# Moving weight conversions out of the projection stages, and conditioning rows between gate stages, in a two-layer decoder trunk

## The chip, the cores and the metric

One Trainium2 chip, eight cores in two dies (cores 0 to 3 and 4 to 7). Each core computes one of eight batch elements; the cores exchange nothing. The time is that of the slowest core, in microseconds of the device.

A run is in one of two states. In a slow one, a die shows a lower granted TensorE clock than the other and is over 1% longer (or the run is over 1.5% above the fastest of the same kernel). I also use the **undisturbed-die time**: the median span of a die's four cores, where their median granted clock was at least 0.9965, averaged over all such dies of all runs of a kernel on one chip.

## The reference, cut to what matters

```python
D_MODEL, BATCH, SEQ, DEPTH, D_FF = 1024, 8, 4096, 2, 2816
for l in range(DEPTH):
    mod = c_act @ ada_w[l] + ada_b[l]              # 9 vectors of 1024: "conditioning rows"
    sh1, sc1, g1, sh2, sc2, g2, sh3, sc3, g3 = jnp.split(mod, 9, axis=-1)
    y = modulate(rmsnorm(h, norm_g[l, 0]), sh1, sc1)
    h = h + 0.5 * g1 * swiglu(y, ffn1_wg[l], ffn1_wu[l], ffn1_wd[l])
    y = modulate(rmsnorm(h, norm_g[l, 1]), sh2, sc2)
    proj = y @ w_in[l]                             # the projection stage
    ...                                            # gating unit || dilated attention
    h = h + g2 * (mixed @ w_out[l])
    y = modulate(rmsnorm(h, norm_g[l, 2]), sh3, sc3)
    h = h + 0.5 * g3 * swiglu(y, ffn2_wg[l], ffn2_wu[l], ffn2_wd[l])
```

All weights arrive as f32. The kernel uses bf16.

## The kernel before: what the change and the argument touch

The kernel describes its work as a graph of tasks. When the program is built, a list scheduler with a model of the DMA gives each engine a fixed order; on the chip only semaphores hold it. So one moved transfer can change the order of every engine.

```python
def schedule(self, bw=270.0, dlat=2300.0, ...):    # the model: 270 bytes/ns, 2.3 us to land
    ...
    if t.dma:
        far = t.L - hp                             # distance to the deadline
        bl = backlog if far < 12000.0 or now < 100000.0 else 5000.0 if far < 40000.0 else 2500.0
        if pipe[0] - now > bl:                     # modelled backlog: hold this transfer back
            ...
            continue
```

A **conversion** is a DMA from DRAM to DRAM issued by GpSimd, which rounds f32 to bf16. It waits only for a matmul, its gate:

```python
def conv(l, w, spans, gates=True):                 # spread over stretches of TensorE's program time
    items = ([(j, None) for j in range(FC)] if gates else []) + [(None, m) for m in range(KC)]
    ...
        gate = max((k for k in marks if k[0] <= p), key=lambda k: k[0], default=(0, None))[1]
        if j is not None:                          # gate-up weights: 22 per FFN
            G.dma("pool", lambda e, j=j: e.dma_start(out=wguS[l, w, j], in_=wgu_d[l, w, j]), 1572864,
                  writes=[bWG[l, w, j]], name="cvg", pos=p, extra=[gate])
        else:                                      # down weights: 8 per FFN
            G.dma("pool", lambda e, m=m: e.dma_start(out=wdS[l, w, m], in_=wd_d[l, w, m]), 2162688, ...)
```

A **conditioning row** (`cond`) loads 512 KB of `ada_w` and multiplies and sums it on VectorE. In a projection stage TensorE multiplies the normalised rows by `w_in`; beside it the next tiles of h are loaded and normalised. Their squares run on ScalarE, in the same queue as the copies that empty PSUM:

```python
def norm_sum(ht, pos, alts=0):
    ...                                            # each kc: ScalarE, needs the load of ht.b[kc]
    G.op([act(lambda e, sq=sq, hk=hk: e.activation(out=sq, in_=hk, func=AF.Square), 520)],
         reads=[ht.b[kc]], writes=[bq], name="sq", pos=pos)
```

The stages of one layer, with 0, p1, ... as TensorE's program time:

```python
f1.gates((0, 1, 2, 3), ...)      # p1 .. pg   first gates
f1.downs(...); f1.downs(...)     # pg .. p2
mx0.proj(t)  # t = 0..3          # p2 .. p3   first projection stage
fa.gates, fa.downs, ...          # p3 .. p4   gates of tiles 4..7, attention woven in
mx1.proj(t); outproj(...)        # p4 .. p6   second projection stage
fb.gates, fb.downs, ...          # p6 .. p7   second FFN, attention woven in
fc.gates((4, 5, 6, 7), ...)      # p8 .. s1   last gates
```

The softmax here doesn't subtract the row's maximum and nothing guards it: scores larger than these inputs give would overflow.

## Time and profile before

| | before |
|---|---|
| first three timed runs | 4849.5, 5211.1, 5432.4 us |
| profiled run (fast) | 4873.3 us |
| TensorE's waits over 0.1 us, median core | 78.8 us, of which 44.2 before the first projection stage |

The last row is mine: for each two successive matmuls of the trace I take the time from start to start, less the pace of an unbroken stream (215.8 ns for 512 columns; the formula is in the prediction), and sum what exceeds 0.1 us. The median is over the six cores whose traces hold every matmul. This sum is small: 1.6% of the span. The views themselves are shown in the prediction.

Two cautions go with it. The cores of one run differ: the six stand at 71.7 to 81.5 us here. And not all of it is waiting. The clock records of the traces show short stretches, often of 3.4 us, in which a core was granted half its clock (0.5); a matmul of 512 columns then takes 0.21 us more, and the sum counts it.

### The profile page before, as it was taken

How to read it: one execution, taken by the hardware profiler on the slowest of the kernel's cores; microseconds unless marked ns; L12 is line 12 of the kernel's file. 1: busy time of each engine (PE TensorE's matmuls, PEld its weight loads, DVE VectorE, ACT ScalarE, POOL GpSimd, SP SyncE). 2: the span in 40 equal slices, each digit the busy share in tenths (PEclk: the TensorE clock that was granted, in tenths of full speed). 3: DMA queues.
4: the chain of work that ended last, by engine and by line, in shares of the span. 5: the costliest groups of instructions: out<-in, count | busy, mean ns of one | idle time of the engine just before them, and what ended most of it. 6: DMA issues, size and time to landing. Idle time of an engine off the chain costs nothing.

```text
span 4871.8 us, 74168 instructions; the slowest of 8 cores (4820.7 to 4871.8 us)
## 1 busy us (share of the span) xinstructions
PE 4789.6 (98%) x25859; PEld 2257.4 (46%) x25859; DVE 2461.2 (51%) x4088; ACT 2035.0 (42%) x3024; POOL 973.5 (20%) x949
## 2 busy tenths in 40 slices
PE   6999999999999999999999999999999999999998
PEld 2444445444445554444444444444444455544443
DVE  6452566473655473655233326645537544525433
ACT  5112576452755352512211127645537444525311
POOL 0001551212531111300100026312235100122101
PEclk9999999999999999999999999999999999999999
DMA  8888676777575768755721466756665644473314
GB/s 240 169 191 230 166 204 159 191 206 218 172 209 150 200 192 240 218 147 165 249 66 39 120 200 163 208 155 184 149 190 164 185 148 140 123 248 124 136 42 157
DMA packets 370033, 834.80 MB, mean 171 GB/s; under 512 B 148961, under 2 KB 182113, under 8 KB 363234
## 3 DMA queue, kind: packets, MB, share of 16 engines
q1 hardware_dynamic: 352338, 741.56, 49.4%
q0 software_dynamic: 17328, 88.49, 12.1%
q8 instruction: 213, 3.49, 0.3%
q14 instruction: 154, 1.26, 0.1%
HBM read 741.20 MB, written 234.88 MB: 200 GB/s over the span
## 4 chain that ended last, share of the span: by engine, by line
PE 92%; ACT 2%; DMA 2%; DVE 2%; issue 1%; POOL 0%; SPq 0%; DVEq 0%; ACTq 0%; POOLq 0%
PE ps L1002 48%; PE ps L1030 25%; PE ps L1141 9%; PE ps L1467 5%; PE ps L1409 3%; PE ps L1375 2%; DMA arena<-xP 1%; DMA arena<-hS 0%; DVE arena L1206 0%; DVE arena L948 0%; POOL arena L1182 0%; DMA arena<-ada_w 0%; ACT arena L1184 0%; DMA arena<-wdS 0%; PE ps L1234 0%
## 5 line engine op out<-in xcount | busy, mean ns | idle before, releaser
L1002 PE MATMUL ps<-arena 128*128 128x512 bf16 x11264 | 2511.5, 381 | 32.6 <-DMA arena<-wgu 25.0
L1002 PEld LDWEIGHTS ps<-arena 128*128 128x128 bf16 x11264 | 1083.9, 98 | 1312.0 <-issue 86.4
L1030 PE MATMUL ps<-arena 128*128 128x512 bf16 x5632 | 1242.7, 382 | 1.1 <-DMA arena<-wdS 1.1
L1008 ACT ACTIVATE arena<-ps 128x512 f32<-128x512 f32 x704 | 419.7, 597 | 1283.7 <-PE ps L1002 1279.9
L1010 DVE SCALAR_TENSOR_TENSOR arena<-arena,ps 128x512 f32<-128x512 f32 x704 | 481.4, 685 | 771.9 <-ACT arena L1008 770.7
L1030 PEld LDWEIGHTS ps<-arena 128*128 128x128 bf16 x5632 | 550.7, 98 | 665.6 <-issue 47.9
L926 POOL TENSOR_TENSOR arena<-arena 128x512 f32<-128x512 f32 (+2 forms) x351 | 414.2, 1180 | 1218.4 <-ACT arena L919 1116.3
L1034 DVE SCALAR_TENSOR_TENSOR arena<-ps,arena 128x512 f32<-128x512 f32 x256 | 192.1, 751 | 908.3 <-PE ps L1030 899.9
L1015 DVE TENSOR_TENSOR arena<-ps,arena 128x512 bf16<-128x512 f32 x704 | 485.0, 690 | 216.6 <-PE ps L1002 193.3
L1141 PE MATMUL ps<-arena 128*128 128x512 bf16 x2560 | 577.1, 385 | 9.0 <-ACT arena L1225 5.8
L919 ACT ACTIVATE arena<-arena 128x512 bf16<-128x512 f32 x424 | 250.9, 625 | 709.1 <-DVE arena L1034 379.3
L1393 ACT ACTIVATE arena<-ps 128x1024 bf16<-128x1024 f32 (+1 forms) x384 | 344.9, 950 | 308.3 <-PE ps L1375 307.6
L1141 PEld LDWEIGHTS ps<-arena 128*128 128x128 bf16 x2560 | 251.0, 99 | 314.7 <-issue 52.0
L1396 DVE TENSOR_TENSOR arena<-arena 128x1024 bf16<-128x1024 bf16 (+1 forms) x384 | 256.1, 675 | 126.0 <-ACT arena L1393 124.6
L961 ACT ACTIVATE arena<-arena 128x512 bf16<-128x512 f32 x372 | 278.4, 806 | 45.2 <-DVE arena L948 45.1
L1445 POOL TENSOR_TENSOR arena<-arena 64x512 bf16<-64x512 f32 x128 | 163.8, 1280 | 623.1 <-ACT arena L1440 600.0
L948 DVE TENSOR_TENSOR arena<-arena 128x512 f32<-128x512 f32 x384 | 268.3, 747 | 35.0 <-ACT arena L934 32.0
L1467 PE MATMUL ps<-arena 128*128 128x512 bf16 x1024 | 230.1, 386 | 0.0
L1425 DVE TENSOR_TENSOR arena<-ps,arena 128x512 f32<-128x512 f32 x256 | 175.5, 685 | 65.2 <-PE ps L1409 57.5
L1409 PEld LDWEIGHTS ps<-arena 128*128 128x128 bf16 x2736 | 173.6, 98 | 63.4 <-issue 7.1
L1213 POOL TENSOR_TENSOR arena<-arena 128x512 bf16<-128x512 f32 x128 | 167.9, 1320 | 174.8 <-DVE arena L1204 120.2
L1409 PE MATMUL ps<-arena 128*128 128x128 bf16 x2736 | 194.4, 219 | 1.9 <-DVE arena L1010 0.9
(79 smaller groups left out, 2112.7 us busy)
## 6 DMA issues: line engine op xcount, KB each, us to landing
arena<-wguS SPq DMA_DIRECT2D x242, 512.0 KB, 5.7
arena<-hS SPq DMA_DIRECT2D x204, 512.0 KB, 6.8
arena<-wdS SPq DMA_DIRECT2D x128, 704.0 KB, 5.9
arena<-ada_w SPq DMA_DIRECT2D x144, 512.0 KB, 5.9
hS<-arena SPq DMA_DIRECT2D x224, 256.0 KB, 5.8
wguS<-wgu POOLq DMA_DIRECT2D x66, 512.0 KB, 7.8
hS<-arena SPq DMA_DIRECT2D x64, 512.0 KB, 4.3
arena<-xP SPq DMA_DIRECT2D x48, 512.0 KB, 9.0
```

Of the source, the lines that this page charges most:

```text
L926: f = lambda e, a=a, sq=sq, out=out: e.tensor_tensor(out=out, in0=a, in1=sq, op=ALU.add)
L948: f = lambda e, hk=hk, u=u: e.tensor_tensor(out=u, in0=hk, in1=rs, op=ALU.mult)
L961: ga = act(lambda e, hk=hk, A=A, sh=sh, o=o: e.activation(out=o, in_=hk, func=AF.Identity, scale=A, bias=sh), 725)
L1002: mate = main([(lambda e, kc=kc, half=half, bk=bk, y=y, gu=gu: e.matmul(bank(bk), lhsT=gu[:, half, kc, :], rhs=y[:, kc, :], start=(kc == 0 ...
L1008: G.op([act(lambda e, sg=sg, gb=gb: e.activation(out=smv[sg.i], in_=bank(gb), func=AF.Tanh, scale=0.5), 490, "tanh")], reads=[gb], writes= ...
L1010: G.op([dve(lambda e, sg=sg, gb=gb: e.scalar_tensor_tensor(out=smv[sg.i], in0=smv[sg.i], scalar=1.0, in1=bank(gb), op0=ALU.add, op1=ALU.mu ...
L1015: G.op([dve(lambda e, sg=sg, ub=ub, o=o: e.tensor_tensor(out=o, in0=bank(ub), in1=smv[sg.i], op=ALU.mult), 610)], reads=[ub, sg], writes=[ ...
L1030: main([(lambda e, j=j: e.matmul(bank(bk), lhsT=wd[:, j, :], rhs=a[:, j, :], start=(j == 0), stop=(j == FC - 1)), [bwd, ba[j]], MM) for j ...
L1141: ins.append((lambda e, lhs=lhs, rhs=rhs, kc=kc: e.matmul(bank(bk), lhsT=lhs, rhs=rhs, start=(kc == 0), stop=(kc == KC - 1)), rd + [by[kc] ...
L1393: return e.activation(out=cut(pT, 0), in_=cut(ps[:, :, :], sb.i * 512), func=AF.Exp, scale=0.125)
L1409: return e.matmul(o, lhsT=v[:, vi, h * 64:h * 64 + 128], rhs=pT[:, h, b, pc, :], start=(pc == 0 or not prev), stop=(pc == 1))
L1467: main([(lambda e, kc=kc, m=m, bk=bk: e.matmul(bank(bk), lhsT=w[:, m, kc, :], rhs=mx[:, kc, :], start=(kc == 0), stop=(kc == KC - 1)), [bw ...
```

## The change

The intent: take the conversions of the second FFN out of the projection stages, which also carry loads of h, rotary tables and stores of q, k and v, and put them, with layer 1's conditioning rows, into gate stages with few transfers. The core of the diff (cut: bookkeeping of the new pacing, and `downs=False` in `conv`):

```diff
+    PFAR, PLEN, PRATE = 1e9, 3000.0, 0.7
...
+                    if far > self.PFAR and now > 100000.0 and pace[0] - now > self.PLEN:
+                        t.held = True
...
-                          name="wins", pos=pos + 60000.0)
+                          name="wins", pos=pos + 240000.0)
...
+            else:
+                conv(l, 0, [(p1 + 20000.0, pg)], False)
+                cond(range(96, 120), (p1 + 30000.0, pg - 20000.0), ...)
...
-            if l == 0:
-                cond(range(48, 72), (p3 + 20000.0, q1 - 20000.0), ...)
+            cond(range(72 * l + 48, 72 * l + 72), (p3 + 20000.0, q1 - 20000.0), ...)
...
-            conv(l, 1, [(p2, p4)])
+            conv(l, 1, [(p1 + 280000.0, pg - 20000.0), (p3 + 10000.0, p4 - 40000.0)] if l == 0 else
+                       [(p1 + 150000.0, pg - 20000.0), (p3 + 10000.0, p4 - 40000.0)])
...
-                cond(range(92, 144), (p8 + 5000.0, s1 - 20000.0), ...)
+                cond(range(92, 96), (p8 + 5000.0, s1 - 20000.0), ...)
...
-                conv(l + 1, 0, [(p6, r3), (p8, s1)])
+                conv(l + 1, 0, [(p6 + 40000.0, r3), (p8 + 60000.0, s1 - 20000.0)], downs=False)
```

More of the change, by code (lines that the diff above doesn't have):

```diff
@@ L112, in _new @@
         t.mate = None
+        t.held = False
         t.banks, t.new = [], []
@@ L227, in schedule @@
         pipe = [0.0]
+        pace = [0.0]
+        pes = []
         port = [0.0]
@@ L332, in pick @@
                         continue
+                    if far > self.PFAR and now > 100000.0 and pace[0] - now > self.PLEN:
+                        t.held = True
+                        nxt = min(nxt, max(pace[0] - self.PLEN, now + 100.0))
+                        continue
                     if pipe[0] - now > 3000.0 and any(x.dma and x.eng is None and x.L < t.L and not x.new
@@ L396, in schedule @@
             t.start, t.dur = st, dur
+            if e == "pe":
+                pes.append(t)
+            if t.dma and t.held:
+                x = next((x for x in reversed(pes) if x.end + 100.0 <= now), None)
+                if x is not None:
+                    t.deps = t.deps | {x}
             if t.dma:
+                pace[0] = min(max(pace[0], now) + t.nbytes / (bw * self.PRATE), max(now + 8000.0, pipe[0] + t.nbytes / bw))
                 pipe[0] = max(pipe[0], st + dur) + t.nbytes / bw
@@ L857, in build_nc, with conv @@
         marks = []
-        def conv(l, w, spans, gates=True):
-            items = ([(j, None) for j in range(FC)] if gates else []) + [(None, m) for m in range(KC)]
+        def conv(l, w, spans, gates=True, downs=True):
+            items = ([(j, None) for j in range(FC)] if gates else []) + ([(None, m) for m in range(KC)] if downs else [])
             wt = [1.0 if m is None else 1.4 for _, m in items]
@@ L1519, in build_nc @@
                 cond(range(16, 48), (p1 + 30000.0, pg - 20000.0), steps(WD0 + 4096, 4096, 3), WD0)
+            else:
+                conv(l, 0, [(p1 + 20000.0, pg)], False)
+                cond(range(96, 120), (p1 + 30000.0, pg - 20000.0), steps(WD0 + 4096, 4096, 3), WD0)
             wdn[0] = 0
@@ L1557, in build_nc @@
             nrm(5, 1, q2 + 40000.0, H)
-            if l == 0:
-                cond(range(48, 72), (p3 + 20000.0, q1 - 20000.0), steps(WD0 + 4096, 4096, 3), WD0)
+            cond(range(72 * l + 48, 72 * l + 72), (p3 + 20000.0, q1 - 20000.0), steps(WD0 + 4096, 4096, 3), WD0)
             wdn[0] = 0
@@ L1578, in build_nc @@
                 norm_y(ht, t - 4, l, 2, G.M, 0, True)
-            conv(l, 1, [(p2, p4)])
+            conv(l, 1, [(p1 + 280000.0, pg - 20000.0), (p3 + 10000.0, p4 - 40000.0)] if l == 0 else [(p1 + 150000.0, pg - 20000.0), (p3 + 10000.0, p4 - 40000.0)])
             sq_more.clear()
@@ L1606, in build_nc @@
             if not last:
-                cond(range(92, 144), (p8 + 5000.0, s1 - 20000.0), steps(WD0 + 4096, 4096, 3), WD0)
+                cond(range(92, 96), (p8 + 5000.0, s1 - 20000.0), steps(WD0 + 4096, 4096, 3), WD0)
                 wdn[0] = 0
```

## The prediction

> **What bounds the kernel now.** I read the table of cores first, then the page's busy line and chain, then busy time by stretch, then TensorE's own waits in the two stages that the change unloads, then the chain there.
>
> ```profile
> core 5: 4871.8 us, clock 0.989
> die 0 (median of its cores): 4824.8 us, clock 0.998
> die 1 (median of its cores): 4864.5 us, clock 0.990
> ```
>
> The profiled run is a fast one: the dies differ by under 1%, and the slower has the lower granted clock. The kernel's three timed runs were 4849.5, 5211.1 and 5432.4 us, so only one of them was fast.
>
> ```profile
> PE 4789.6 (98%) x25859; PEld 2257.4 (46%) x25859; DVE 2461.2 (51%) x4088; ACT 2035.0 (42%) x3024; POOL 973.5 (20%) x949
> PE 92%; ACT 2%; DMA 2%; DVE 2%; issue 1%; POOL 0%; SPq 0%; DVEq 0%; ACTq 0%; POOLq 0%
> ```
>
> Matmuls are 98% of the span and 92% of the chain. Since busy time overstates pipelined matmuls, I check the rate: the chain of waits has one unbroken piece of 1264 matmuls (line L1002) in 272.81 us, 215.8 ns each. At that rate the weight matmuls alone, 11264 (L1002) + 5632 (L1030) + 2560 (L1141) + 1024 (L1467) = 20480, need 4420 us. The attention matmuls come on top. What is left to win is the time in which TensorE stands still, and that is short. Its waits over the whole span, longest sums:
>
> ```profile
> PE ps L1002 <- DMA arena<-wgu: 25.0, 3, 22.3
> PE ps L930 <- DVE arena L926: 7.7, 2, 5.4
> PE ps L775 <- DVE arena L771: 6.6, 1, 6.6
> PE ps L1141 <- ACT arena L1225: 5.8, 3, 2.5
> PE ps L1002 <- DVE arena L954: 4.3, 3, 1.8
> PE ps L1234 <- POOL arena L1182: 3.7, 2, 1.9
> ```
>
> The first, third and fifth, and most of the second, belong to the start of the kernel, which the change does not touch. The fourth and sixth belong to the projection stages. Next the stretches of the parts concerned. The columns are length, then busy time of PE, PEld, DVE, ACT and POOL with counts, granted clock, DMA share, GB/s.
>
> ```profile
> 55.00:362.00 307.00, 303.31 (x1397) 136.48 (x1396) 169.99 (x271) 85.68 (x135) 18.50 (x35) 1.00 0.85 186
> 517.00:669.00 152.00, 146.01 (x705) 66.46 (x704) 108.19 (x248) 117.69 (x194) 98.41 (x89) 0.99 0.71 168
> 669.00:1150.00 481.00, 478.28 (x3026) 235.89 (x3025) 278.58 (x446) 254.81 (x369) 90.68 (x92) 0.99 0.74 192
> 1996.00:2302.00 306.00, 306.00 (x1402) 137.98 (x1401) 184.07 (x297) 83.05 (x132) 32.57 (x32) 0.99 0.60 166
> 2460.00:2764.00 304.00, 304.00 (x1410) 137.81 (x1409) 121.39 (x176) 53.83 (x89) 5.32 (x10) 1.00 0.18 50
> 2919.00:3071.00 152.00, 145.05 (x698) 66.20 (x696) 108.04 (x247) 117.25 (x193) 98.23 (x89) 0.99 0.62 166
> 3071.00:3594.00 523.00, 521.74 (x3239) 255.87 (x3238) 259.94 (x402) 265.83 (x380) 106.15 (x107) 1.00 0.68 177
> ```
>
> In order: first gate stage of layer 0, its first projection stage, gates with attention, the last gate stage of layer 0 (second FFN), then layer 1's first gates, first projection, gates with attention. The reader should see two things. TensorE idles 6.0 us and 7.0 us in the projection stages and 2.7 us and 1.3 us in the attention stages. It idles not at all in 1996:2302, although conversions and conditioning rows take part of the DMA there, and the transfers of layer 1's first gates leave 82% of the DMA free. The chain shows how one projection stall arises:
>
> ```profile
> 2955.02 7.97 DMA arena<-hS
> ...
> 2963.62 0.17 ACT arena L919
> ...
> 2964.14 0.58 ACT arena L1225
> ```
>
> A load of h takes 7.97 us to land. The square of the norm (L919) stands at the head of ScalarE's in-order queue and waits for it. Behind it stands the copy (L1225) that empties a PSUM bank, and TensorE waits for the bank.
>
> **What the Trainium skill says.** "Trainium Kernel Development and Optimization", section Performance Expectations, calls matmul busy time a bad metric because matmuls are pipelined; that is why I used the rate. "TensorE: Matmul & The Clock Gate", section "Wait — 56ns, not 53.3ns?", gives N ÷ 2.4 GHz + about 2.5 ns, 215.7 ns at N = 512; the 215.8 ns above agree. "DMA: Bandwidth & Descriptors", section "Issuing engines are not separate DMA queues", says transfers issued by the sync and GpSimd engines run on the same 16 DMA engines and interleave. So a conversion issued from GpSimd does compete with loads of h, and moving it moves load rather than removing it; the trace agrees in so far as GpSimd's queue holds 17.4% of the DMA time in 517:669 beside 53.4% for the other. The clock page, section "Part 1: The HAM clock gate (the "warmup" mystery)", describes a current limit that takes a die to 13/16 of the clock under dense matmuls on three or more cores. The 0.989 of core 5 is consistent with short episodes of it; no run so far shows what ended or began one.
>
> **The change part by part.** First, what is inert. The pacing code added to the scheduler acts only when a transfer's deadline is more than 1e9 ns away; the whole program is under 5e6 ns, so it never acts. The position of the winS store (60 us to 240 us later) is not used either: a position sets the deadline only of operations that nobody depends on, and this store has dependents. For conversions, the position only selects the matmul that releases them; for conditioning rows it is the place in the program, hence when their buffers are free, that matters.
>
> (a) Conversions of the second FFN leave the projection stages. The DMA listing shows 7 gate-up conversions in each. In 517:669 GpSimd's queue takes 17.4% of 152 us, 26.4 us of all 16 engines, or 3.8 us per conversion. The DMA share falls from 0.71 to about 0.54, and in layer 1 from 0.62 to about 0.46 (that queue had 16.4%). Gain: only waits for loads of h can shrink. Of the TensorE waits in layer 0's stage, 3.2 us are on L1225; in layer 1's, 2.5 us on L1225 and 2.5 on L1157, another ScalarE copy in the same queue. That is 8.2 us. Loads landed in 5.6 to 8 us in the chain there; the quickest listed medians for such loads elsewhere are 5.3 us. So I take half: 4 us. The two waits on L1182 (1.9 and 1.8 us) follow six short GpSimd normalisations held up by VectorE's rope work, not by a conversion, and stay.
>
> (b) They go into the gates with attention. In layer 0 that stage held 15 gate-up and 5 down conversions, and gets nearly all 30: 7 x 0.524 + 3 x 0.721 = 5.8 MB more written. GpSimd's queue took 20.2% of 481 us for 13.57 MB, 7.2 us per MB, so +42 us, and the share rises from 0.74 to about 0.83. In layer 1, about 8 of the 30 fit into the first gates (134 of 540 us of program time), and the attention stage keeps about as many as before. Cost: the 0.85 of 55:362 was carried with hardly a wait, but that stage has no attention. The waits in 669:1150 include one of 1.1 us for a down weight (L1030 from wdS). I allow 2 us.
>
> (c) 48 of layer 1's conditioning rows leave 1996:2302; 24 go to layer 1's first gates and 24 to its attention gates. A row is 512 KB and one VectorE instruction of 1.22 us. 12.6 MB at the 3.2 us per MB of the other queue (35.2% of 272 us for 30.2 MB in 90:362) is 40 us of DMA per 24 rows, and 24 x 1.3 = 31 us of VectorE with the accumulator read. Layer 1's first gates go from 0.18 to about 0.18 + 0.13 (rows) + 0.14 (8 down conversions, 5.8 MB) + 0.10 (8 gate-up conversions) = 0.55; VectorE from 121 to about 152 of 304 us. Its attention stage goes from 0.68 to about 0.76, VectorE from 260 to 291 of 523. That is the load which layer 0's stage carries now with 24 rows (0.74; 279 of 481) at 2.7 us of idle against 1.3. Cost: 1 us. The stage they leave has no wait to lose. Gain: 0.
>
> (d) Two more copies of the conditioning vector: each a 512 KB load, a ScalarE instruction of 1.05 us with perhaps a table load of 1.28 us, a VectorE instruction of 1.22 us, all in gate stages with idle time. Cost: 0.
>
> Sum: -4 + 2 + 1 = -1 us, on 4849.5. I predict 4849 us for a fast run.
>
> **The rivals.**
> 1. Full relief: all 8.2 us go, and the new places absorb everything; about 4841 us. For: 2460:2764 is nearly empty. Against: the square waits for its load also when the DMA is quiet, since loads are issued only after the buffer is free.
> 2. Overload: at about 0.83 mean share the attention gates of layer 0 see weight loads land late, several waits like the 1.1 us one; at 5 to 15 us, 4855 to 4865 us. Also, conversions stand in GpSimd's in-order queue, each waiting for a matmul, and can hold the attention's normalisation behind them. For: GpSimd already waits 255.2 + 230.1 us for matmuls at the gate-up conversions. Against: attention's GpSimd results are needed only by the output projection.
> 3. A reshuffled static order: conversions change the build-time order of every engine, so a new unlucky head-of-queue wait of 2 to 5 us can appear anywhere, in either direction.
> 4. Clock: 53 us of core 5's span are its missing 1.1% of clock. If calmer projection stages draw differently, that could exceed all of the above, but nothing in the trace says which way.
>
> **Range and chances.** A 2% gain needs 97 us, more than all TensorE waits of the listing together, so faster by over 2% has a chance of 1%. Slower by over 2% needs a starved stage; 2%. Within 2%: 97%, fast runs against fast runs. Lower end: 4800, since fast runs of one kernel already differ by 0.5% here (4849.5, and 4873.3 for the profiled one) and rival 1 comes on top. Upper end: 5220, since two of three recorded runs were slow and a median of a few runs may again be a slow one; for fast runs alone I would say 4885. The point, 4849, is that of a fast run.
>
> **What would show it.** Right: no gate-up conversion issued inside the two projection stages; DMA shares there near 0.54 and 0.46; waits on L1225 and L1157 halved, L1182's unchanged; 0.83 in layer 0's attention gates with TensorE idle below 5 us; about 0.55 in layer 1's first gates with none. Wrong: idle over 10 us in an attention stage, a new wait for a weight load above 2 us, or projection waits unchanged although the DMA share fell (then the loads were late for another reason). A fast run outside 4820 to 4885 us would mean that a wait I did not list governs.

## The result, and the profile after

The changed kernel's median is 5125.2 us over six runs (4847.5 to 5493.5), that of the kernel before 4915.7 over six (4846.8 to 5432.4). Both medians mix states. The fast runs against the fast runs give a ratio of 0.9994, 95% interval 0.9972 to 1.0017: the same time within 2%. (A ratio is the mean time of one kernel's fast runs over that of the other's fast runs of the same rounds, so not quite the ratio of medians.)

Behind that "same" stands a small real gain. A second job on another chip gave the undisturbed-die time of both: 4828.2 us before (6 dies, 4827.4 to 4829.4) and 4817.5 us after (8 dies, 4815.5 to 4818.6). The change is worth 10.7 us, 0.22%. The first ratio hides most of it, since die 1 of that chip ran at a clock of 0.99 even in fast runs:

```profile
core 5: 4846.0 us, clock 0.992
die 0 (median of its cores): 4817.7 us, clock 0.998
die 1 (median of its cores): 4842.5 us, clock 0.992
```

Next the stretches of the changed kernel. The first six answer to those shown of before in the same order, without the first gates of layer 0 (TensorE busy 303.1 of 307 us, against 303.3 before); the seventh is layer 0's second projection stage. Columns as in the prediction.

```profile
516.00:663.00 147.00, 146.20 (x701) 67.06 (x700) 111.13 (x247) 105.62 (x178) 102.32 (x92) 0.97 0.53 156
663.00:1145.00 482.00, 481.31 (x3058) 237.86 (x3056) 277.98 (x446) 262.39 (x374) 91.56 (x96) 1.00 0.84 194
1988.00:2290.70 302.70, 302.70 (x1404) 137.20 (x1403) 132.34 (x195) 83.60 (x134) 28.22 (x29) 1.00 0.27 74
2445.00:2749.00 304.00, 304.00 (x1410) 137.84 (x1409) 149.18 (x229) 54.82 (x90) 13.79 (x27) 1.00 0.57 128
2903.00:3050.00 147.00, 147.00 (x701) 67.44 (x699) 111.40 (x247) 105.42 (x178) 102.19 (x92) 0.97 0.51 156
3050.00:3572.00 522.00, 520.27 (x3238) 255.35 (x3237) 284.07 (x455) 265.33 (x378) 103.11 (x103) 1.00 0.77 194
1145.00:1392.50 247.50, 244.57 (x1149) 111.13 (x1147) 139.84 (x293) 136.25 (x222) 121.44 (x110) 0.97 0.76 202
```

The same second projection stage before:

```profile
1150.00:1400.00 250.00, 249.20 (x1173) 113.46 (x1172) 141.45 (x294) 138.91 (x227) 118.06 (x105) 0.97 0.66 197
```

Three things are to be seen. Both first projection stages are full: TensorE idles 0.8 and 0.0 us, where it idled 6.0 and 7.0. Layer 0's attention gates carry a DMA share of 0.84 and idle no more than before. But the second projection stage, which I had not written about, got a share of 0.76 instead of 0.66 and idles 2.9 us instead of 0.8. Six of layer 0's eight down conversions are issued there (from 1132 to 1283 us); before it was three or four (1124 to 1218).

TensorE's waits after, those that answer to the list before:

```profile
PE ps L1017 <- DVE arena L969: 25.9, 4, 22.1
PE ps L945 <- DVE arena L941: 7.0, 2, 4.7
PE ps L790 <- DVE arena L786: 6.5, 1, 6.5
PE ps L1017 <- DMA arena<-wgu: 3.1, 2, 1.9
PE ps L1017 <- DMA arena<-wguS: 1.7, 1, 1.7
PE ps L1249 <- ACT arena L1199: 1.7, 4, 0.6
PE ps L1156 <- ACT arena L1240: 0.8, 1, 0.8
```

These line numbers are all 15 higher than before: L1017, L1156, L1240 and L1199 were L1002, L1141, L1225 and L1184. The first four waits are the start of the kernel (part of the second its end), as before; the longest is now put down to another last releaser. The waits of the projection on the copy L1225 have shrunk from 5.8 to 0.8 us. The wait of 3.7 us on GpSimd's normalisation (L1182), which I had said would stay, is below 0.4 us.

By stage, in us of TensorE's waits over 0.1 us, medians over complete cores (the after column is the second job's):

| stage | before | after |
|---|---|---|
| first projection, layer 0 / layer 1 | 7.4 / 5.5 | 0.8 / 0.4 |
| attention gates, layer 0 / layer 1 | 2.6 / 2.3 | 1.8 / 3.0 |
| layer 0: second projection + second FFN | 2.1 + 2.0 | 4.0 + 5.0 |
| layer 1: second projection + the rest | 1.8 + 9.7 | 1.7 + 6.1 |
| all | 78.8 | 67.0 |

The total falls by 11.8 us, and the undisturbed die by 10.7: the waits account for the change.

### The profile page after: what moved, and what is told of

Its sections match the earlier page's. It is cut to its first block, busy times and chain, and to the rows that moved or that the text cites. A ratio compares the mean times of both kernels' runs of the same rounds, so it can differ in the third digit from the quotient of the medians.

```text
span 4846.0 us, 74149 instructions; the slowest of 8 cores (4812.7 to 4846.0 us)
## 1 busy us (share of the span) xinstructions
PE 4774.6 (99%) x25859; PEld 2254.5 (47%) x25859; DVE 2462.6 (51%) x4090; ACT 2018.6 (42%) x2996; POOL 983.1 (20%) x967
## 4 chain that ended last, share of the span: by engine, by line
PE 93%; DMA 2%; ACT 2%; DVE 1%; issue 1%; POOL 0%; DVEq 0%; SPq 0%; ACTq 0%; POOLq 0%
PE ps L1017 48%; PE ps L1045 25%; PE ps L1156 10%; PE ps L1482 5%; PE ps L1424 3%; PE ps L1390 2%; DMA arena<-xP 1%; DMA arena<-wdS 1%; DMA arena<-wguS 0%; DMA qS<-arena 0%; ACT arena L1023 0%; PE ps L1249 0%; PE ps L945 0%; DVE arena L963 0%; DVE arena L985 0%
## 5 line engine op out<-in xcount | busy, mean ns | idle before, releaser
L1017 PE MATMUL ps<-arena 128*128 128x512 bf16 x11264 | 2503.6, 380 | 32.3 <-DVE arena L969 25.9
L1017 PEld LDWEIGHTS ps<-arena 128*128 128x128 bf16 x11264 | 1082.1, 98 | 1306.3 <-issue 63.8
L1156 PE MATMUL ps<-arena 128*128 128x512 bf16 x2560 | 575.6, 385 | 0.9 <-ACT arena L1240 0.8
L1156 PEld LDWEIGHTS ps<-arena 128*128 128x128 bf16 x2560 | 252.2, 99 | 305.6 <-issue 39.0
L976 ACT ACTIVATE arena<-arena 128x512 bf16<-128x512 f32 x372 | 279.7, 808 | 46.2 <-DVE arena L963 45.6
L963 DVE TENSOR_TENSOR arena<-arena 128x512 f32<-128x512 f32 x384 | 278.3, 773 | 35.3 <-ACT arena L949 32.0
L1228 POOL TENSOR_TENSOR arena<-arena 128x512 bf16<-128x512 f32 x128 | 171.0, 1349 | 192.4 <-DVE arena L1219 128.8
```

The source lines that it names most:

```text
L963: f = lambda e, hk=hk, u=u: e.tensor_tensor(out=u, in0=hk, in1=rs, op=ALU.mult)
L976: ga = act(lambda e, hk=hk, A=A, sh=sh, o=o: e.activation(out=o, in_=hk, func=AF.Identity, scale=A, bias=sh), 725)
L1017: mate = main([(lambda e, kc=kc, half=half, bk=bk, y=y, gu=gu: e.matmul(bank(bk), lhsT=gu[:, half, kc, :], rhs=y[:, kc, :], start=(kc == 0 ...
L1156: ins.append((lambda e, lhs=lhs, rhs=rhs, kc=kc: e.matmul(bank(bk), lhsT=lhs, rhs=rhs, start=(kc == 0), stop=(kc == KC - 1)), rd + [by[kc] ...
```

## The experiments

Two theories. **Contention**: the conversions' traffic in the projection stage made loads of h land late, and removing the traffic removed the waits. **Re-planning**: the scheduler, seeing fewer transfers, put the engines' work in a better order, and the order removed the waits. Beside them, GpSimd's in-order queue as a carrier, the down conversions left over into the second projection as the cause of the new waits there, and overload of the attention gates.

I built the kernel before with the pacing code and the moved winS position alone. Its instructions and waits are identical on all five engines, so those parts of the diff are inert, as predicted.

In this table, waits are in us, medians over complete cores, and the last column is the undisturbed-die time less that of the kernel before on the same chip (4 to 8 dies for each kernel). The dies of one kernel lie 2 to 10 us apart, and the cores of one run differ by some us in a projection stage, so differences of 1 or 2 us are within the spread. x_late has no row: all its runs were slow.

| kernel | first proj. L0 / L1 | attention L0 / L1 | L0: 2nd proj. + 2nd FFN | all waits | die time |
|---|---|---|---|---|---|
| before (first profile) | 7.4 / 5.5 | 2.6 / 2.3 | 4.1 | 78.8 | 0 |
| e_after (the change) | 0.8 / 0.4 | 1.8 / 3.0 | 9.0 | 67.0 | -10.7 |
| e_conv | 1.0 / 2.0 | 1.8 / 2.9 | 8.5 | 73.0 | -4.9 |
| e_rest | 9.0 / 5.3 | 2.7 / 2.9 | 4.2 | 78.2 | -1.2 |
| x_late2 | 5.9 / 5.2 | 4.9 / 8.6 | 4.8 | 86.8 | +10.2 |
| x_early | 12.3 / 6.0 | 1.9 / 2.8 | 6.9 | 82.5 | +4.4 |
| x_sp | 12.4 / 6.1 | 1.8 / 2.9 | 7.3 | 83.0 | +8.5 |
| x_pool | 0.8 / 0.9 | 1.7 / 2.9 | 7.3 | 66.7 | -9.9 |
| x_spill | 0.9 / 0.2 | 9.4 / 2.8 | 8.5 | 74.4 | -6.3 |
| x_double | 0.8 / 0.6 | 60.9 / 25.1 | 37.6 | 189.1 | none clean |
| e_rev | 0.5 / 0.0 | 1.2 / 2.6 | 6.3 | 65.7 | -11.2 |
| e_dfb | 1.4 / 2.6 | 2.7 / 2.6 | 24.2 | 86.7 | +4.6 |

**The change again, beside the next three.** The unchanged file.

> The changed kernel again, on the same chip as the next three. Fast runs within 0.4% of the kernel before; on a die that keeps its clock its cores should be 5 to 12 us shorter than before's (the first pair of profiles: die 0 4824.8 against 4817.7 us). TensorE's waits in the first projection stages of both layers below 2 us each (before: 5 to 9 us), and 4 to 8 us of waits in the second projection stage of layer 0 and the start of its next gates.

Measured: as expected, by the table. The ratio of fast runs was 0.9903 with an interval from 0.9762 to 1.0045, so unclear by itself: five of the seven runs of before in that job were slow, and one of the two fast ones had die 1 at 0.988. The undisturbed dies decide.

**One part alone: the second FFN's conversions.**

```diff
-            conv(l, 1, [(p2, p4)])
+            conv(l, 1, [(p1 + 280000.0, ...), (p3 + 10000.0, p4 - 40000.0)] if l == 0 else [...]   # in before
```

> Kernel before with one part of the change: the second FFN's conversions leave the projection stages. If they alone explain it (both theories, contention and re-planning, say so, since the scheduler plans anew here): projection waits below 2 us each in both layers, and the spill of down conversions into layer 0's second projection stage with 4 to 8 us of waits there. Rival, that the moved conditioning rows matter: the waits of layer 1's projection stay at 5 to 8 us. Total within 0.3% of before in fast runs.

Measured: layer 0 as after, 1.0 us. Layer 1 keeps 2.0 us, less than before, more than after. The new waits in layer 0's second projection and FFN are all there (8.5 us). Die time -4.9 us.

**The rest alone.** The changed kernel with `conv(l, 1, [(p2, p4)])` put back.

> The changed kernel with the second FFN's conversions put back over the projection and attention stages: only rows and layer 1's first down conversions move. If the conversions are what matters: projection waits again 5 to 9 us in each layer, as before, no gain; total within 0.3% of before. Rival, rows matter: layer 1's projection waits fall below 3 us.

Measured: the projection waits are back (9.0 and 5.3 us). Die time -1.2 us, which is within the spread (dies at 4825.3 to 4828.9 us against 4827.4 to 4829.4). So the relief of the projection belongs to the conversions. The two parts together give more (-10.7) than the sum of each alone (-6.1): with static orders, parts don't add up.

**The old order without the traffic.** From here on, edits are made after scheduling. The orders of TensorE, VectorE, ScalarE and SyncE stay exactly those of the kernel named; I compared the instruction lists. First attempt:

```diff
         G.schedule()
+        for l in range(DEPTH):
+            c = convs(l, 1, "g")                  # in before: gate-up conversions of the second FFN
+            for k in range(7):                    # those of the projection stage ...
+                G.order.remove(c[k])
+                G.order.insert(G.order.index(c[7 + k]) + 1, c[k])    # ... issued later
```

> Kernel before with the order of TensorE, VectorE, ScalarE and SyncE untouched; only the seven conversions of each projection stage are issued later by GpSimd, in the attention stage. Contention theory: the waits for late loads of h in the projection stages (on the ScalarE copies, 3.2 and 5.0 us on the slowest core) fall by more than half, the waits on GpSimd's normalisation (1.9 and 1.8 us) stay; sum 2 to 4 us per stage. Re-planning theory: the order is the same, so the waits stay at 5 to 8 us per stage.

Measured: every run was slow, so its time says nothing. Die 1 kept its clock in the profile (0.994), and there the three complete cores waited 6.7 to 8.9 us in layer 0's projection and 5.2 to 6.7 in layer 1's. Contention had said 2 to 4. But the edit had a flaw: it made a burst. In a stretch of 60 us, ten conversions took 21.8 us each to land (median), and TensorE waited 20.9 us at one go for a load of v:

```profile
PE ps L1412 <- DMA arena<-vS: 36.6, 2, 20.9
```

So I repeated it without the burst, one conversion behind each of the last seven:

```diff
+                G.order.insert(G.order.index(c[15 + k]) + 1, c[k])
+                c[k].deps = set(c[15 + k].deps)
```

> Kernel before, order of TensorE, VectorE, ScalarE and SyncE untouched; the seven conversions of each projection stage are issued after the middle of the attention stage, one behind each of the last seven gate-up conversions, so without the burst that the first attempt had. If the first attempt's reading holds (with the old order the projection waits do not need the conversions' traffic), they stay at 4 to 8 us per stage with a DMA share near 0.53; if traffic makes them, below 2 us. Without the burst, no wait over 5 us on the loads of v; attention waits below 6 us.

Measured, core 5, the stretch of layer 0's first projection and its waits:

```profile
514.00:666.00 152.00, 147.38 (x728) 68.07 (x727) 109.95 (x251) 120.21 (x198) 99.15 (x85) 1.00 0.52 158
```

```profile
PE ps L1237 <- POOL arena L1185: 1.9, 1, 1.9
PE ps L1144 <- ACT arena L1160: 1.5, 1, 1.5
```

The DMA share is as low as in the changed kernel (0.52), yet TensorE still idles 4.6 us; the medians over the cores are 5.9 and 5.2 us. That is 1.5 and 0.3 us less than before, and the cores overlap: in layer 0 they stood at 4.5 to 9.3 us before and stand at 4.4 to 8.3 us here. Core 5 alone would half support contention: its waits on the copy L1228 (L1225 before) fell from 3.4 to 1.1 us. But over all cores, the listed waits on ScalarE's two copies that contention was to explain (L1225 and L1157 before) stay at a median of 2.8 us in layer 0. **Contention alone is refuted**: with the old order, the projection waits do not need the conversions. One expectation failed: the attention stages, which took the conversions, wait 4.9 and 8.6 us, where I had allowed 6; most of the +10.2 us of die time is there.

**The new order with the traffic.** The reverse: seven conversions put back into each first projection stage of the changed kernel, behind matmuls 17.9 us apart.

```diff
+            for k in range(7):
+                put(c[k], mark(P2[l] + 17900.0 * k), "pool")   # in after; nothing else moves
```

> Changed kernel with the order of TensorE, VectorE, ScalarE and SyncE untouched; only GpSimd issues seven conversions of the second FFN inside each first projection stage again, 17.9 us apart as before. Contention theory: waits of 3 to 6 us come back in each projection stage. Re-planning theory: the new order bears it, waits stay below 2 us.

Measured: 12.3 and 6.0 us of waits. Core 5 in layer 0's projection, the stretch and its longest waits:

```profile
542.40:702.00 159.60, 148.31 (x702) 67.66 (x701) 110.53 (x247) 104.09 (x177) 105.78 (x99) 0.97 0.65 166
```

```profile
PE ps L1159 <- ACT arena L1243: 3.1, 2, 2.7
PE ps L1252 <- ACT arena L1202: 3.0, 1, 3.0
PE ps L948 <- POOL arena L944: 2.9, 1, 2.9
```

Not only do they come back, layer 0's median is larger than before (12.3 against 7.4 us; the cores reach from 4.4 to 16.7 us). 2.6 us of it are matmuls at half clock. **Re-planning alone is refuted too**: the new order is good only while these transfers are away.

**Which carrier?** The changed kernel with plain copies of the same source size by SyncE, and the changed kernel with tiny converting copies by GpSimd, at the same places:

```diff
+  extra("sp",   ... dma_start(out=dumS[l, k], in_=wgu_d[l, 1, k]) ...)                  # x_sp, 1 MB each
+  extra("pool", ... dma_start(out=dumS[l, k], in_=wgu_d[l, 1, k, :, 0, 0, 0:16]) ...)   # x_pool, 4 KB written
```

> Changed kernel, same order, plus seven plain 1 MB DRAM-to-DRAM copies per projection stage issued by SyncE at the same places: the DMA load of the conversions without GpSimd. If DMA traffic makes the waits, they come back as in the run with seven conversions put back (3 to 6 us); if GpSimd's queue makes them, they stay below 2 us.

> Changed kernel, same order, plus seven tiny converting copies (4 KB written) per projection stage issued by GpSimd at the same places and behind the same matmuls: GpSimd's queue time and wait without the DMA load. If GpSimd's queue makes the waits, 3 to 6 us come back; if DMA traffic does, they stay below 2 us.

Core 5 in layer 0's projection: the stretch and its longest waits with SyncE's copies, then all waits with GpSimd's tiny ones.

```profile
512.80:671.40 158.60, 146.90 (x702) 67.29 (x701) 111.04 (x247) 104.37 (x177) 102.06 (x92) 0.98 0.69 190
```

```profile
PE ps L1160 <- ACT arena L1244: 3.4, 1, 3.4
PE ps L949 <- POOL arena L945: 3.1, 1, 3.1
PE ps L1253 <- ACT arena L1203: 2.8, 1, 2.8
```

```profile
PE ps L1160 <- ACT arena L1244: 1.5, 1, 1.5
PE ps L1253 <- POOL arena L1201: 0.5, 1, 0.5
```

SyncE's copies make the same waits as the conversions (12.4 and 6.1 against 12.3 and 6.0); GpSimd's tiny ones make none (0.8 and 0.9). The loads of x in 517:669, with SyncE's copies and then with the tiny ones (median us to landing last):

```profile
arena<-xP SPq DMA_DIRECT2D x11, 512.0 KB, 9.8
arena<-xP SPq DMA_DIRECT2D x12, 512.0 KB, 6.1
```

Over five cores these medians are 8.8 to 10.6 us and 5.3 to 6.6 us. The carrier is the DMA engines' time, not GpSimd's queue. SyncE's copies also stand in the queue that issues the loads, but the conversions by GpSimd do not, and their harm is the same.

**Where the order differs.** ScalarE's and SyncE's rows in time, before and then after; columns are start, length, engine, line, operation.

```profile
538.69 3.56 ACT L1184 ACTIVATE arena<-arena 128x128 bf16<-128x128 f32 x9
551.06 5.74 ACT L961 ACTIVATE arena<-arena 128x512 bf16<-128x512 f32 x8
552.70 4.59 SPq L897 DMA_DIRECT2D arena<-hS  x4
```

```profile
542.20 5.74 ACT L976 ACTIVATE arena<-arena 128x512 bf16<-128x512 f32 x8
543.84 4.60 SPq L912 DMA_DIRECT2D arena<-hS  x4
```

The next tile of h is loaded into the buffer that the eight instructions L961 (now L976) read to make the normalised outputs, so the load has to wait for them. Before, nine small normalisations of the gating unit (the first row) stand in ScalarE's queue ahead of the norm's own logarithm and exponential, which those eight need (the exponential runs at 547.47 us, after the change at 539.01). So the eight begin at 551.06 us instead of 542.20, and the load goes out at 552.70 instead of 543.84. The stages began at 517.1 and 515.9, so 7.7 us of the 8.9 are the order's. In x_late2, which has the old order and the emptier DMA, the square still waits for this load (1.30 us), and a copy and TensorE wait behind it:

```profile
555.27 1.15 ACT L922 ACTIVATE arena<-arena 128x512 bf16<-128x512 f32 x2 [1.30 <-DMA arena<-hS]
557.54 4.76 PE L1144 MATMUL ps<-arena 128*128 128x512 bf16 x20 [1.53 <-ACT arena L1160]
```

This is one place of several: before the change it holds 1.1 us of core 5's 6.0. What the new order did to the others was not traced.

That the scheduler chose otherwise because its DMA model was emptier is argued, not shown: I did not log its choices.

**The left-over down conversions.** In the changed kernel, the six issued in the second projection stage are issued among the gate-up conversions of the attention stage, with the gates of those.

```diff
+        for k in range(2, 8):                     # shortened
+            G.order.remove(c[k]); c[k].deps = set(g[2 * k + 5].deps)
+            G.order.insert(G.order.index(g[2 * k + 5]) + 1, c[k])
```

> Changed kernel, same order; only the six down conversions that were issued in layer 0's second projection stage (1132 to 1283 us) are issued earlier, among the gate-up conversions of the attention stage. If their traffic makes the new waits there: waits between 1130 and 1420 us fall from 5 to 7 us to below 3 us, DMA share there from 0.76 to about 0.64, and the attention stage stays below 5 us of waits at a share near 0.9. Rival: the waits there come with the new order and stay.

Measured, core 5, the second projection:

```profile
1145.00:1392.50 247.50, 245.87 (x1178) 113.02 (x1176) 141.18 (x295) 137.35 (x224) 122.42 (x108) 0.99 0.61 187
```

The DMA share there falls from 0.76 to 0.61, but the median waits of the stage and of the next FFN stay: 3.7 + 4.8 us against 4.0 + 5.0. The attention stage goes from 1.8 to 9.4 us, where I had allowed 5. My theory falls: the new waits in layer 0's second half do not come with the left-over traffic. The scheduler's holding back was even of use.

How much the order does is seen in the five runs that share it (e_after and the x_ runs made from the changed kernel, without x_double). The second FFN waits 4.7 to 5.1 us in all of them, against 2.0 before: these 3 us are the order's. The second projection is not so steady: 2.2 to 4.0 us against 2.1 before. Four of x_spill's cores stand there at 3.6 to 3.7 us and two at 2.2, and on the four the clock records show a stretch of 3.4 us at half clock. What brings that stretch on stays open, so 3 of the 4.9 us are shown to be the order's, and the rest is not.

**Overload.** Every conversion of the second FFN from the attention stage on is issued twice, the copy into scratch.

```diff
+                    d = G.dma("pool", lambda e, src=src, dst=dst: e.dma_start(out=dst, in_=src), t.nbytes, name="dum")
+                    G.order.insert(G.order.index(t) + 1, d)
```

> Changed kernel, same order; every conversion of the second FFN that is issued from the attention stage on is issued twice, the copy into scratch. Tests the overload rival: if the attention stage has reserve at a share of 0.84, waits there stay below 6 us per layer; if it is at its limit, the share goes towards 1.0 and TensorE waits 20 us or more in layer 0's attention stage, less in layer 1's (0.77). My guess: 30 us and 10 us.

Core 5, layer 0's attention stage, and its longest waits:

```profile
657.00:1209.00 552.00, 493.73 (x3060) 241.67 (x3057) 279.45 (x447) 262.59 (x374) 106.96 (x122) 0.95 0.91 193
```

```profile
PE ps L1429 <- DVE arena L1416: 28.6, 3, 15.2
PE ps L1050 <- DMA arena<-wdS: 10.8, 1, 10.8
```

A share of 0.84 was borne with 1.8 us of waits, 0.91 costs 61 us (my guess was 30), and layer 1's stage 25 us. The overload rival did not come true at the change's dose, but the reserve was small. How much of this is the mean load and how much the pairing of conversions, these runs don't separate; the first attempt above shows that a burst alone suffices.

**Two tries at a better version.** Down conversions ahead of gate-up conversions:

```diff
+            if w == 1:
+                items = items[FC:] + items[:FC]
```

> Changed kernel with the down conversions of the second FFN ahead of its gate-up conversions, planned anew. If the six down conversions left over into the second projection stage cost the 4 to 5 us of waits that came new there and in the next gates, these fall to about 4 us together and the kernel is 3 to 5 us shorter on an undisturbed die (4812 us); if the new waits come with the order, they differ by chance, 2 to 10 us.

Measured: 65.7 us of waits in all and -11.2 us, against 67.0 and -10.7 of the change: no difference that the spread of the dies (4814.2 to 4823.8 us) would let me claim. And layer 0's down conversions moved on into the second FFN's gates:

```diff
+            if l == 0:                            # and downs=False in its other conv(l, 1, ...)
+                conv(l, 1, [(p6, p6 + 100000.0)], gates=False)
```

> Changed kernel with layer 0's eight down conversions of the second FFN moved on into the first gate stage of that FFN, planned anew. Tries for a version better than both: attention and second projection stage of layer 0 lose 8 conversions (share there near 0.76 and 0.64), the next gates gain them. Expected on an undisturbed die 4810 to 4820 us (changed kernel 4815 to 4818); over 4825 if the gates cannot take them.

Measured: worse, +4.6 us. The stage that received them waits 21.3 us instead of 5.0. No version that clearly beats the changed kernel was found.

## Why the prediction was right or wrong, point by point

**The step that failed is the gain of (a): "only waits for loads of h can shrink", "so I take half: 4 us", and the two waits on L1182 "stay".** I had read the chain as contention, that is, load late, square late, copy late. The waits fell from 7.4 + 5.5 to 0.8 + 0.4 us, by 11.7. Taking the traffic away without a new order saved 1.8 us, no more than the spread of the cores; only the new order with the emptier DMA saved the rest, including the waits on GpSimd's normalisation (L1182) that I had excluded. At the place traced, the load was late because it was issued late, and the order did that. The shares themselves came out at 0.53 and 0.51, where I had 0.54 and 0.46.

**The step from the sum to the point failed too: "The point, 4849, is that of a fast run."** The fast runs were 4847.5 and 4848.8 us, and 4844.9 in one more, so it holds for what it says, though partly by luck: the sum behind it was 10 us off on undisturbed dies, and die 1 of that chip, which set the time, ran at 0.99 in both kernels' profiles. But the recorded time is a median over runs of all states: 5211 us before, when I predicted, and 5125.2 after, from four slow runs and two fast ones. Beside 5211, a point of 4849 says -7%, which my own sum (-1 us) never supported; the ratio of fast runs is 0.9994. The prediction had noted that two of three runs before were slow and used it only for the upper end. A point in the terms of that median would have been 5210.

**Inert parts**: right, shown by identical instruction lists.

**(b) Cost in layer 0's attention gates, 2 us**: the share, 0.83, was right (0.84); the cost was not there (2.6 to 1.8 us). "Gets nearly all 30" was wrong: six down conversions slid on. The cost came elsewhere, +4.9 us in layer 0's second projection and second FFN. About 3 us of it are shown to be the order's, as the third rival had it in kind and size (2 to 5 us).

**(c) Rows, 1 us**: right. Layer 1's first gates reached 0.57 (0.55 predicted) with VectorE at 149 us (152) and no wait; its attention gates reached 0.77 (0.76) and wait 3.0 instead of 2.3 us. **(d)**: no wait was found that belongs to the two extra copies.

**The sum**: -1 us predicted, -10.7 us measured on undisturbed dies. The nearest rival was the first, full relief at -8.2 us, though not by its mechanism. Of the 3.6 us gained in the rest of layer 1, where hardly a transfer moved, about 1.2 are matmuls at half clock that the first profile had and the later one not; the others I put down to re-planning, but that is not shown: both the change and the rest alone have the gain (6.1 and 6.7 against 9.7 us), the conversions alone less (8.3). The outcome fell where the 97% stood, within 2%. On the clock, the fourth rival, the traces now say what the 0.989 was: short stretches at 13/16 (last section).

## What to carry to other kernels

In a statically ordered kernel, ask of a late load when it was issued before asking what slowed it: a transfer blamed in the chain may be late by the order of another engine, and then moving traffic away helps only through the new order. Separate the two by editing the emitted order after scheduling, in both directions, and compare 0.2% effects by waits per stage and by dies that kept their clock.

## What the Trainium skill lacked or had wrong

- "TensorE: Matmul & The Clock Gate", section "Part 1: The HAM clock gate (the "warmup" mystery)": it says that a die with three or more cores on dense matmuls goes to 13/16 of the clock within 5 to 20 us and stays there while the load lasts. Here all eight cores ran dense matmuls, and the undisturbed dies of fast runs kept a mean of 0.998 for 4.8 ms. The clock records of die 1 in the first profile of before (mean 0.99) show 13/16 in 35 to 42 stretches of 3.7 to 9.1 us for each core, 195 to 244 us in all. In the slow run that was profiled (x_late), die 0 was granted it for 3.9 to 4.0 of 5.5 ms. Slow runs had means from about 0.98 down to 0.814 on a die (5796.4 us for that die). So 13/16 does occur, but neither always nor for as long as the load lasts; no run shows what begins or ends a stretch.
- "DMA: Bandwidth & Descriptors", section "Issuing engines are not separate DMA queues": right that queues of different engines interleave on the same DMA engines, and the plain copies by SyncE did the harm of GpSimd's conversions. It lacks a size for what interleaving costs a load: on core 5, 512 KB loads of x landed in a median of 6.1 us with tiny extra copies and 9.8 us with seven 1 MB copies per projection stage. In a burst, ten conversions landed in a median of 21.8 us, and TensorE waited 20.9 us for a load of v from the other queue.
